# Summing the modulations' partial products on four column groups at once, with two accumulators

## The chip, the cores and the metric

The kernel runs on one core of a Trainium2 chip. The metric is the time on the device of one execution, in microseconds (us). TensorE multiplies matrices, VectorE and ScalarE work element by element, GpSimd does a few small things, and SyncE issues most of the DMAs. In the profile they are PE (PEld is its loading of weights), DVE, ACT, POOL and SP. Each engine takes its instructions strictly in the order in which the program lists them for it. An instruction waits for a semaphore where it needs another engine's result or a buffer that another engine still uses.

## The reference

The model is a hybrid of two layers over 512 tokens (256 of context, 256 latent) of 1024 channels. Every layer has nine modulation vectors for each of the two streams; the latent tokens are modulated by `c`, the context tokens by `c_ctx`:

```python
for l in range(DEPTH):                                  # DEPTH = 2
    ml = jnp.split((jax.nn.silu(c) @ ada_w[l] + ada_b[l])[:, None, :], N_MOD, axis=-1)
    mc = jnp.split(jax.nn.silu(c_ctx) @ ada_w[l] + ada_b[l], N_MOD, axis=-1)
    h = h + 0.5 * ml[2] * _swiglu(_modulate(_rms(h, ffn1_norm[l]), ml[0], ml[1]), ffn1_w13[l], ffn1_w2[l])
    ...                                                 # the context stream hc alike, with mc
    y_lat, y_ctx = _mixer(_modulate(_rms(h, mix_norm[l]), ml[3], ml[4]), ...)
    h = h + ml[5] * y_lat
    h = h + 0.5 * ml[8] * _swiglu(_modulate(_rms(h, ffn2_norm[l]), ml[6], ml[7]), ffn2_w13[l], ffn2_w2[l])
return _rms(h, final_norm)                              # of the latent stream
```

The change touches only how `silu(c) @ ada_w[l]` and `silu(c_ctx) @ ada_w[l]` are computed. One modulation is 1024 channels of two streams: for each stream a vector of 1024 numbers times a matrix of 1024 x 1024.

## The kernel before

**Stages.** The program runs through the two layers in order: first FFN of layer 0 (in the profiled execution until about 425 us), mixer of layer 0 (to about 1080), second FFN of layer 0 (to about 1455), first FFN of layer 1 (to about 1850), mixer of layer 1 (to about 2320), second FFN of layer 1. Activations lie with the channels on the partitions. Every large product (`mm3`, line 142) is made of three float32r products for each k tile of 128 channels: high part by high part, low by high, high by low. A weight tile of 1024 x 128 comes by one DMA of SyncE's queue (`raw`), ScalarE rounds it to its high part (`whi`, line 112), VectorE subtracts that from the raw tile for the low part (`wlo`, line 113), and TensorE then uses it for 24 products (8 k tiles by 3) of 512 columns. `whi` and `wlo` have three buffers each, so ScalarE can start on a tile when TensorE has left the tile three places earlier.

**Modulations.** Modulations 0 and 1 of layer 0 are made at the very start by TensorE (`ada_now`). The other sixteen (2 to 8 of layer 0, 0 to 8 of layer 1) are made beside the products of the FFNs by `ada`: seven in the first FFN of layer 0, six in its second, three in the first FFN of layer 1. A modulation is eight jobs. `beside` hands the jobs out evenly over 64 calls of `weights()`, so about one job follows each weight tile. A job loads 256 rows by 512 columns of `ada_w` (`adaw`, line 286, from the same pool of three buffers and the same SyncE queue as `raw`), and VectorE multiplies each row of it by the number of `silu(c)` for its partition and adds it up: `aacc` [128 partitions, 2 streams, 512 columns], two operations of line 293 for the first k tile and fourteen of line 295 for the other seven. Four jobs make one half (`r` = 0 or 1) of a modulation's 1024 columns.

What is then left is the sum over the 128 partitions. TensorE does it: a product with a 128 x 32 block of ones (line 301) puts the sum of every column on 32 rows of PSUM. A half has two such products, one for each stream, on the column groups `g = 2 * s + r` of the array (four groups of 32 columns); half 0 uses groups 0 and 2, and half 1 groups 1 and 3 of the same PSUM tile. The operands are plain float32, and each such product shows as two MATMUL records of 32 columns by 512 in the trace. After half 1 `modulation` copies the PSUM tile (ScalarE, line 239), transposes it in four pieces (TensorE, line 242), and VectorE adds the bias (line 249) and prepares the scales.

`aacc` has a single buffer (`bgp` is a pool of one). So the first operation of a half on VectorE cannot start before TensorE has done the previous half's two products:

```python
if k == 0:
    st.acc = self.bgp.tile([128, 2, 512], F32, tag="aacc", name="aacc")
...
if k == 6:
    if r == 0:
        st.ps = self.psx()
    for s in range(2):
        g = 2 * s + r
        nc.tensor.matmul(st.ps[32 * g:32 * g + 32, :], lhsT=self.ones[:, :32], rhs=st.acc[:, s],
                         start=True, stop=True, tile_position=(0, 32 * g))
```

**Order.** The order on each engine is settled when the program is built, by a scheduler of the framework that goes by the order of emission and by priorities; the two parts of a weight tile have a higher priority than the jobs. The order on SyncE's queue decides when weights and `ada_w` blocks are loaded.

**A relative.** `sums` in the mixer (line 931) does a sum over the partitions too, with the same shape of product (`sel`, 128 x 32, by 512 columns in plain float32), and issues four of them one behind the other on the four column groups. It is not changed, and its rows stand below as line 931.

## Time and profile before

| | |
|---|---|
| three runs | 2528.02, 2529.99, 2535.90 us |
| median of the runs | 2529.99 us |
| profiled execution: span from its first to its last instruction | 2526.3 us |
| profiled execution: what lies around the span | not recorded; the lowest run is 1.7 us above the span, the median 3.7 us |
| PE busy | 2427.5 us (96%) |
| DVE busy | 1776.3 us (70%) |
| ACT busy | 956.2 us (38%) |
| PE records of line 301 | 128, 37.1 us busy |
| DVE on the accumulations, lines 293 and 295 | 64 and 448 operations |

Busy time is the union of an engine's instructions. Matmuls overlap one another in the records (a product of 512 columns shows as some 0.39 us, and the next one starts 0.23 us later), so the time that TensorE spends on something is read from starts, not from the durations. In the rows below a timeline line gives the start in us from the start of the span, the length, the engine, the line of the program, the operation, what it writes and reads, the count of merged records, and in brackets how long the engine was idle before and what ended that.

### The profile page before, as it was taken

Reading aid. Unit: us, or ns where it says so; the run is one execution under the profiler, and the core shown is the slowest. Engines: PE = TensorE matmul, PEld = TensorE weight load, DVE = VectorE, ACT = ScalarE, POOL = GpSimd, SP = SyncE. Lnnn points to the kernel's source line nnn. Section 1 sums busy time; section 2 is a strip of 40 time slices with the busy share of each in tenths; the row PEclk is TensorE's granted clock in tenths of the full one; section 3 lists DMA queues with packets and bytes.
Section 4 is the critical chain, followed back from the end, with each engine's and each line's share of the span. In section 5 each row is a group of like instructions: output and inputs, shape, how many; then the busy total and the mean of one; then the engine's idle time right before and its main releaser. Section 6 shows DMA issues by size and latency. Waiting matters only on the chain. (4 is left out here: it accounts for less than half of the span.)

```text
span 2526.3 us, 38353 instructions
## 1 busy us (share of the span) xinstructions
PE 2427.5 (96%) x15099; PEld 2044.0 (81%) x15099; DVE 1776.3 (70%) x3023; ACT 956.2 (38%) x1578; POOL 51.5 (2%) x111
## 2 busy tenths in 40 slices
PE   7999999999999999999999999999988998978998
PEld 5777778787887887887777887777887897978998
DVE  4766767699999676576666564445468998966554
ACT  3222222435443643332222232222244556544443
POOL 0000000100000000000000000000010000000000
PEclk9999999999999999999999999999998998999999
DMA  8555555743653465355555544444466572356664
GB/s 252 167 162 166 172 174 175 167 134 109 209 142 115 144 217 161 119 151 161 158 153 163 152 118 126 125 125 127 127 163 180 168 212 82 94 186 174 196 185 137
DMA packets 566773, 394.61 MB, mean 156 GB/s; under 512 B 27704, under 2 KB 513218, under 8 KB 564930
## 3 DMA queue, kind: packets, MB, share of 16 engines
q1 hardware_dynamic: 555606, 371.33, 50.0%
q0 software_dynamic: 2304, 8.39, 1.7%
q10 hardware_dynamic: 8684, 12.45, 1.4%
q8 instruction: 118, 1.93, 0.3%
q14 instruction: 61, 0.50, 0.1%
HBM read 358.43 MB, written 33.69 MB: 155 GB/s over the span
## 5 line engine op out<-in xcount | busy, mean ns | idle before, releaser
L142 PE MATMUL pm<-nh,whi 128*128 128x512 f32 (+1 forms) x2544 | 910.6, 360 | 21.2 <-ACT whi L112 14.5
L142 PE MATMUL pm<-nh,wlo 128*128 128x512 f32 (+1 forms) x2544 | 905.4, 357 | 2.8 <-DVE wlo L113 2.2
L142 PE MATMUL pm<-nl,whi 128*128 128x512 f32 (+1 forms) x2544 | 905.9, 357 | 0.0
L112 ACT ACTIVATE whi<-raw 128x1024 fp32r<-128x1024 f32 (+1 forms) x450 | 469.0, 1044 | 1150.5 <-PE pm L142 892.4
L113 DVE TENSOR_TENSOR wlo<-raw,whi 128x1024 fp32r<-128x1024 f32 (+1 forms) x450 | 540.9, 1203 | 273.7 <-ACT whi L112 270.1
L142 PEld LDWEIGHTS pm<-nh,whi 128*128 128x128 f32 x2544 | 482.2, 190 | 121.7 <-ACT whi L112 32.5
L142 PEld LDWEIGHTS pm<-nh,wlo 128*128 128x128 f32 x2544 | 482.4, 190 | 79.8 <-DVE wlo L113 4.5
L142 PEld LDWEIGHTS pm<-nl,whi 128*128 128x128 f32 x2544 | 482.7, 190 | 73.1 <-DVE nl L376 1.0
L295 DVE SCALAR_TENSOR_TENSOR aacc<-adaw,sc,aacc 128x512 f32<-128x512 f32 x448 | 311.7, 746 | 111.7 <-DMA adaw<-ada_w_in 111.6
L825 DVE SCALAR_TENSOR_TENSOR cy<-cx,cdw,cy 128x512 f32<-128x512 f32 (+1 forms) x480 | 272.0, 612 | 1.3
L142 PE MATMUL pm<-gh,whi 128*128 128x512 f32 (+1 forms) x770 | 269.6, 350 | 1.7 <-DVE h L381 1.7
L142 PE MATMUL pm<-gl,whi 128*128 128x512 f32 (+1 forms) x770 | 267.6, 348 | 0.0
L142 PE MATMUL pm<-gh,wlo 128*128 128x512 f32 (+1 forms) x770 | 267.1, 347 | 0.0
L142 PEld LDWEIGHTS pm<-gh,whi 128*128 128x128 f32 x770 | 145.7, 189 | 30.5 <-ACT whi L112 6.7
L142 PEld LDWEIGHTS pm<-gl,whi 128*128 128x128 f32 x770 | 145.7, 189 | 18.4 <-issue 0.8
L142 PEld LDWEIGHTS pm<-gh,wlo 128*128 128x128 f32 x770 | 145.7, 189 | 18.1
L429 DVE TENSOR_TENSOR silu<-silu,pm 128x512 f32<-128x512 f32 (+1 forms) x88 | 54.5, 620 | 109.3 <-PE pm L142 100.9
L381 DVE SCALAR_TENSOR_TENSOR h<-pm,gate,h 128x256 f32<-128x256 f32 x80 | 36.5, 480 | 63.9 <-PE pm L142 63.6
L375 ACT ACTIVATE nh<-t,mods 128x256 fp32r<-128x256 f32 x88 | 39.9, 502 | 60.5 <-DVE t L372 60.4
L112 ACT ACTIVATE gh<-silu 128x512 fp32r<-128x512 f32 (+1 forms) x88 | 50.4, 573 | 12.1 <-DVE silu L429 12.1
L113 DVE TENSOR_TENSOR gl<-silu,gh 128x512 fp32r<-128x512 f32 (+1 forms) x88 | 54.4, 618 | 0.0
L142 PE MATMUL pm<-mh,whi 128*128 128x256 f32 (+1 forms) x152 | 47.9, 317 | 2.9 <-ACT mh L112 2.9
(248 smaller groups left out, 2382.6 us busy)
## 6 DMA issues: line engine op xcount, KB each, us to landing
raw<-ffn_w_in SPq DMA_DIRECT2D x208, 512.0 KB, 3.9
adaw<-ada_w_in SPq DMA_DIRECT2D x144, 512.0 KB, 4.4
raw<-w_in_in SPq DMA_DIRECT2D x130, 512.0 KB, 4.3
raw<-ffn_w_in SPq DMA_DIRECT2D x64, 448.0 KB, 4.2
R<-grow POOLq DMA_DIRECT2D x16, 512.0 KB, 13.6
raw<-conv_proj_in SPq DMA_DIRECT2D x16, 512.0 KB, 6.3
raw<-dn_proj_in SPq DMA_DIRECT2D x16, 512.0 KB
raw<-w_out_in SPq DMA_DIRECT2D x16, 512.0 KB, 4.0
```

Source lines behind the costliest of these rows:

```text
L112: nc.scalar.activation(out=hi, in_=x, func=AF.Copy)
L113: nc.vector.tensor_tensor(out=lo, in0=x, in1=hi.bitcast(F32), op=ALU.subtract)
L142: nc.tensor.matmul(ps, lhsT=u[:, j, :], rhs=v[:, k, tok], start=k == 0 and p == 0, stop=k == n - 1 and p == 2)
L295: nc.vector.scalar_tensor_tensor(out=st.acc[:, s], in0=wt[:, j], scalar=c, in1=st.acc[:, s], op0=ALU.mult, op1=ALU.add)
L375: nc.scalar.activation(out=nh[:, k, st], in_=t1, func=AF.Identity, bias=B)
L381: self.nc.vector.scalar_tensor_tensor(out=self.h[:, m, st], in0=ps[:, st], scalar=y.gate[:, q, m, s:s + 1], in1=self.h[:, m, st], op0=ALU. ...
L429: nc.vector.tensor_tensor(out=t, in0=t, in1=pb[:, tok], op=ALU.mult)
L825: nc.vector.scalar_tensor_tensor(out=dst, in0=src, scalar=w, in1=dst, op0=ALU.mult, op1=ALU.add)
```

## The change

Half 0 no longer issues its two products. Both halves keep their accumulator (`st.accs`), for which the tag `aacc` gets two buffers, and after half 1 all four products are issued in a row, on groups 0 to 3: half 0 and half 1 of stream 0, then half 0 and half 1 of stream 1. The PSUM tile is taken only there. (The file of the changed kernel also lost its comments; that moves the line numbers by one and changes nothing else.)

```diff
             if k == 0:
-                st.acc = self.bgp.tile([128, 2, 512], F32, tag="aacc", name="aacc")
+                st.acc = self.bgp.tile([128, 2, 512], F32, tag="aacc", name="aacc", bufs=2)
+                st.accs.append(st.acc)
...
-            if k == 6:
-                if r == 0:
-                    st.ps = self.psx()
-                for s in range(2):
-                    g = 2 * s + r
-                    nc.tensor.matmul(st.ps[32 * g:32 * g + 32, :], lhsT=self.ones[:, :32], rhs=st.acc[:, s],
+            if k == 6 and r == 1:
+                ps = self.psx()
+                for g in range(4):
+                    nc.tensor.matmul(ps[32 * g:32 * g + 32, :], lhsT=self.ones[:, :32], rhs=st.accs[g % 2][:, g // 2],
                                      start=True, stop=True, tile_position=(0, 32 * g))
-                if r == 1:
-                    self.modulation(y, (m,), st.ps, 0, 512, lambda pt: ...)
+                self.modulation(y, (m,), ps, 0, 512, lambda pt: ...)
...
-            st = SimpleNamespace()
+            st = SimpleNamespace(accs=[])
```

The change moves instructions on PE and DVE. On SP and POOL the order is the same as before, row for row, and on ACT six operations change places with a neighbour. On every engine the number of instructions is the same.

On PE, at the end of the first modulation that is made this way (modulation 2 of layer 0), this stands before; `aacc_825` is the accumulator of half 1, and half 0 has its own pair 97 rows earlier:

```order
L142 MATMUL pm_896<-nl_222,whi_899 128x512
L142 MATMUL pm_896<-nh_221,wlo_900 128x512
L301 MATMUL px_789<-aacc_825,ones_89 32x512 x2
L142 MATMUL pm_938<-nh_221,whi_941 128x512
L142 MATMUL pm_938<-nl_222,whi_941 128x512
```

And this stands there now:

```order
L142 MATMUL pm_893<-nl_222,whi_896 128x512
L142 MATMUL pm_893<-nh_221,wlo_897 128x512
L301 MATMUL px_948<-aacc_663,ones_89 32x512
L301 MATMUL px_948<-aacc_822,ones_89 32x512
L301 MATMUL px_948<-aacc_663,ones_89 32x512
L301 MATMUL px_948<-aacc_822,ones_89 32x512
L142 MATMUL pm_935<-nh_221,whi_938 128x512
L142 MATMUL pm_935<-nl_222,whi_938 128x512
```

The four stand at the same place among the products of line 142 as the pair of half 1 did (the numbers of the buffers differ by three), and where the pair of half 0 stood products of line 142 now follow one another. In fifteen of the sixteen modulations the four stand together so.

The sixteenth is modulation 8 of layer 0, at the end of the first FFN, where products of 256 columns run. Before, half 0 has a pair as elsewhere, and the two products of half 1 stand apart, on PE:

```order
L142 MATMUL pm_3061<-gh_611,whi_3076 128x256
L301 MATMUL px_2966<-aacc_2977,ones_89 32x512
L142 MATMUL pm_3061<-gl_612,whi_3076 128x256
L142 MATMUL pm_3061<-gh_611,wlo_3077 128x256
L142 MATMUL pm_3061<-gh_611,whi_3076 128x256
L142 MATMUL pm_3061<-gl_612,whi_3076 128x256
L142 MATMUL pm_3061<-gh_611,wlo_3077 128x256
L301 MATMUL px_2966<-aacc_2977,ones_89 32x512
L142 MATMUL pm_3061<-gh_611,whi_3088 128x256
```

Now the second and third of the four stand together and the fourth a little later, with the first (not in these rows) 34 rows ahead of the second:

```order
L142 MATMUL pm_3058<-gh_611,wlo_3074 128x256
L301 MATMUL px_3095<-aacc_2974,ones_89 32x512
L301 MATMUL px_3095<-aacc_2850,ones_89 32x512
L142 MATMUL pm_3058<-gh_611,whi_3073 128x256
L142 MATMUL pm_3058<-gl_612,whi_3073 128x256
L142 MATMUL pm_3058<-gh_611,wlo_3074 128x256
L142 MATMUL pm_3058<-gh_611,whi_3073 128x256
L142 MATMUL pm_3058<-gl_612,whi_3073 128x256
L301 MATMUL px_3095<-aacc_2974,ones_89 32x512
```

So in this modulation the products of line 301 interrupt the others three times now, and three times before (a pair and two single ones).

On DVE, between the halves of the first modulation, this stands before (`aacc_663` is half 0, `aacc_825` half 1):

```order
L295 SCALAR_TENSOR_TENSOR aacc_663<-adaw_783,sc_135,aacc_663 128x512 x3
L113 TENSOR_TENSOR wlo_820<-raw_817,whi_819 128x1024
L429 TENSOR_TENSOR silu_771<-silu_771,pm_734 128x512
L113 TENSOR_TENSOR wlo_863<-raw_860,whi_862 128x1024
L113 TENSOR_TENSOR gl_612<-silu_771,gh_611 128x512
L293 TENSOR_SCALAR aacc_825<-adaw_823,sc_135 128x512 x2
L295 SCALAR_TENSOR_TENSOR aacc_825<-adaw_823,sc_135,aacc_825 128x512 x2
L295 SCALAR_TENSOR_TENSOR aacc_825<-adaw_866,sc_135,aacc_825 128x512 x4
```

And this stands there now (`aacc_822` is half 1):

```order
L296 SCALAR_TENSOR_TENSOR aacc_663<-adaw_783,sc_135,aacc_663 128x512 x3
L294 TENSOR_SCALAR aacc_822<-adaw_820,sc_135 128x512
L113 TENSOR_TENSOR wlo_817<-raw_814,whi_816 128x1024
L294 TENSOR_SCALAR aacc_822<-adaw_820,sc_135 128x512
L296 SCALAR_TENSOR_TENSOR aacc_822<-adaw_820,sc_135,aacc_822 128x512 x2
L428 TENSOR_TENSOR silu_771<-silu_771,pm_734 128x512
L296 SCALAR_TENSOR_TENSOR aacc_822<-adaw_863,sc_135,aacc_822 128x512
L113 TENSOR_TENSOR wlo_860<-raw_857,whi_859 128x1024
```

Half 1's operations move up to stand directly behind half 0's, ahead of a product with `silu` and of one or two splits of weight tiles.

## Rows read from the trace of the kernel before

**Rows 1.** The page: busy time, share and instructions of each engine.

```profile
PE 2427.5 (96%) x15099; PEld 2044.0 (81%) x15099; DVE 1776.3 (70%) x3023; ACT 956.2 (38%) x1578; POOL 51.5 (2%) x111
```

**Rows 2.** Windows in three FFNs: stretch, length, each engine's busy time, clock, DMA.

```profile
60.00:296.00 236.00, 236.00 (x1015) 182.69 (x1014) 166.06 (x240) 66.13 (x86) 0.00 (x0) 1.00 0.55 164
1080.00:1350.00 270.00, 269.37 (x1207) 211.25 (x1207) 180.74 (x264) 78.00 (x103) 1.07 (x1) 1.00 0.52 154
1440.00:1710.00 270.00, 268.07 (x1291) 218.28 (x1290) 141.15 (x201) 81.25 (x111) 1.83 (x2) 1.00 0.42 123
```

**Rows 3.** Waits of PE from 60 to 425 us: us, times, longest.

```profile
PE px L301 <- DVE aacc L295: 1.4, 2, 0.8
```

**Rows 4.** Waits of all engines over the span.

```profile
ACT whi L112 <- PE pm L142: 892.4, 281, 8.9
DVE aacc L295 <- DMA adaw<-ada_w_in: 111.6, 55, 4.5
DVE aacc L293 <- PE px L301: 18.2, 11, 3.9
```

**Rows 5.** The tile aacc: records of line 301 and line 295, min/median/max in ns.

```profile
L295 DVE SCALAR_TENSOR_TENSOR aacc<-adaw,sc,aacc x448: 737/745/754, 64.4 to 1805.9; 128x512 f32<-128x512 f32 x150
L301 PE MATMUL px<-aacc,ones x128: 589/593/617, 84.0 to 1810.6; 128*32 128x512 f32 x128
```

**Rows 6.** Timeline of PE around the first pair.

```profile
83.48 0.39 PE L142 MATMUL pm<-nl,whi 128*128 128x512 f32 x1
83.71 0.39 PE L142 MATMUL pm<-nh,wlo 128*128 128x512 f32 x1
84.03 1.05 PE L301 MATMUL px<-aacc,ones 128*32 128x512 f32 x4
...
85.35 0.39 PE L142 MATMUL pm<-nl,whi 128*128 128x512 f32 x1
```

**Rows 7.** Timeline of PE around a single product, the first of modulation 8's half 1.

```profile
416.14 0.28 PE L142 MATMUL pm<-gh,whi 128*128 128x256 f32 x1
416.35 1.04 PE L301 MATMUL px<-aacc,ones 128*32 128x512 f32 x2
...
417.55 0.28 PE L142 MATMUL pm<-gh,wlo 128*128 128x256 f32 x1
417.67 0.28 PE L142 MATMUL pm<-gh,whi 128*128 128x256 f32 x1
```

**Rows 8.** Timeline of PE around four products together, line 931, twice.

```profile
571.67 0.39 PE L142 MATMUL pm<-nh,wlo 128*128 128x512 f32 x1
571.99 2.16 PE L931 MATMUL px<-sq,sel 128*32 128x512 f32 x8
...
574.42 0.39 PE L142 MATMUL pm<-nl,whi 128*128 128x512 f32 x1
...
596.35 0.39 PE L142 MATMUL pm<-nh,wlo 128*128 128x512 f32 x1
596.67 1.07 PE L931 MATMUL px<-sq,sel 128*32 128x512 f32 x8
...
598.01 0.40 PE L142 MATMUL pm<-nl,whi 128*128 128x512 f32 x1
```

**Rows 9.** Timeline of PE: the four pairs of a half 0 that took longer.

```profile
345.62 1.62 PE L301 MATMUL px<-aacc,ones 128*32 128x512 f32 x4 [0.67 <-DVE aacc L295]
...
394.83 1.62 PE L301 MATMUL px<-aacc,ones 128*32 128x512 f32 x4 [0.76 <-DVE aacc L295]
...
1104.63 1.49 PE L301 MATMUL px<-aacc,ones 128*32 128x512 f32 x4
...
1402.49 1.64 PE L301 MATMUL px<-aacc,ones 128*32 128x512 f32 x4
```

**Rows 10.** Timeline of ACT and DVE: the two parts of one weight tile.

```profile
78.36 1.06 ACT L112 ACTIVATE whi<-raw 128x1024 fp32r<-128x1024 f32 x1 [3.99 <-PE pm L142]
79.46 1.23 DVE L113 TENSOR_TENSOR wlo<-raw,whi 128x1024 fp32r<-128x1024 f32 x1 [0.45 <-ACT whi L112]
```

More of the change, by code (lines that the diff above doesn't have):

```diff
@@ L295, in job @@
                         nc.vector.scalar_tensor_tensor(out=st.acc[:, s], in0=wt[:, j], scalar=c, in1=st.acc[:, s], op0=ALU.mult, op1=ALU.add)
-            if k == 6:
-                if r == 0:
-                    st.ps = self.psx()
-                for s in range(2):
-                    g = 2 * s + r
-                    nc.tensor.matmul(st.ps[32 * g:32 * g + 32, :], lhsT=self.ones[:, :32], rhs=st.acc[:, s],
+            if k == 6 and r == 1:
+                ps = self.psx()
+                for g in range(4):
+                    nc.tensor.matmul(ps[32 * g:32 * g + 32, :], lhsT=self.ones[:, :32], rhs=st.accs[g % 2][:, g // 2],
                                      start=True, stop=True, tile_position=(0, 32 * g))
-                if r == 1:
-                    self.modulation(y, (m,), st.ps, 0, 512, lambda pt: pt.rearrange("p (j s g r) -> p g j s r", j=4, s=2, g=2)[:, :, :, :, 0])
+                self.modulation(y, (m,), ps, 0, 512, lambda pt: pt.rearrange("p (j s g r) -> p g j s r", j=4, s=2, g=2)[:, :, :, :, 0])
         jobs = []
         for m in mods:
-            st = SimpleNamespace()
+            st = SimpleNamespace(accs=[])
             jobs += [lambda m=m, r=r, k=k, st=st: job(m, r, k, st) for r in range(2) for k in (0, 2, 4, 6)]
```

## The prediction, made before the changed kernel ran

> **What bounds the kernel now.** I read the page's busy times first: TensorE is busy in 96% of the span, VectorE in 70% [rows 1]. A share over the whole span mixes FFNs with mixers, so next I took windows inside the three FFNs in which the sixteen modulations are made: TensorE is busy for 236.0 of 236 us, 269.4 of 270 and 268.1 of 270, at a granted clock of 1.00 throughout (its full 2.4 GHz), with VectorE at 166, 181 and 141 us and the DMA engines at 0.42 to 0.55 [rows 2]. The reader is to see that TensorE is the bound of these stretches and that nothing else is near it. The waits say the same from the other side: in the first FFN TensorE waited 1.4 us for an accumulator, and the answer has only one other row, of 0.6 us [rows 3]; ScalarE stood 892 us, in 281 pieces, waiting for TensorE to leave a weight buffer [rows 4]. Weights are ready ahead of TensorE, not behind it. So an instruction taken off TensorE there moves the end of the kernel by its whole cost, and the work of the accumulation on VectorE lies beside.
>
> Since matmul records overlap, a cost on TensorE is read from starts. I call one interruption of the products of line 142 by products of another shape a **break**, and measure it from the start of the last product ahead of it to the start of the second product behind it, less two ordinary steps. (The second one, because the step after the first product behind is still longer than usual.)
>
> **What one break costs.** Ordinary steps: 83.48 to 83.71, so 0.23 us for 512 columns [rows 6]; 417.55 to 417.67, 0.12 us for 256 columns [rows 7].
> - A pair of line 301: 83.71 to 85.35 is 1.64, less 0.46, is 1.18 us [rows 6].
> - A single product of line 301: 416.14 to 417.55 is 1.41, less 0.24, is 1.17 us [rows 7].
> - Four products of the same shape on four column groups, line 931: 596.35 to 598.01 is 1.66, less 0.46, is 1.20 us [rows 8].
>
> These are the rows on which the forecast rests: one, two or four products cost the same. A break costs 1.2 us, whatever it holds, as long as all operands are there when it begins. Where they are not, it costs more: the other four of line 931 stretched over 2.16 us because two of them came late, 571.67 to 574.42 is 2.75, less 0.46, is 2.29 us, that is 1.09 us more [rows 8].
>
> One rule of the Trainium skill weighs against issuing four: in "TensorE: Matmul & The Clock Gate", section "The cost: per-tile semaphore tail", the tail of a packed group grows by about 4.7 ns for a tile and 26.3 ns for each increment. Two more products with an increment each would by that page make a four dearer than a pair by an estimated 62 ns, 1.0 us for all sixteen, where the rows show 0.02 us; the sum would be 20.3 us instead of 21.0. The rows are of the same shape on the same engine, and I go by them.
>
> **The change part by part.**
> 1. *Breaks on TensorE.* Line 301 has 128 records [rows 5], two for a product, so 64 products. By the order on PE they make 33 breaks before: 31 pairs and two single ones (both of modulation 8 of layer 0). After, they make 18: fifteen fours, and modulation 8's four in three pieces. 15 breaks fewer, at 1.18 us, are 17.7 us. All lie in the FFNs, where TensorE is the bound, so they lie on the path.
> 2. *Fours for pairs.* A four is 0.02 us dearer than a pair; fifteen of them add 0.3 us.
> 3. *Stalls at half 0.* Four pairs of a half 0 took longer than the usual 1.05 us, because the last accumulations came only as TensorE arrived: 1.62 after 0.67 idle, 1.62 after 0.76 idle, 1.49 and 1.64 [rows 9]. The excess is 0.57 + 0.67, 0.57 + 0.76, 0.44 and 0.59, in sum 3.6 us. After the change TensorE doesn't come to half 0 at all at these points, so this goes too, unless the lateness is carried on to the four at the end of half 1. It should not be: TensorE now comes to line 301 only at half 1's place, about four weight tiles later, and half 1 need not wait for half 0's products any more. Before, every half had to wait for those of the half ahead, and VectorE stood 18.2 us in 11 places because of that [rows 4]. Now only the first half of a modulation has to, and on VectorE half 1 stands directly behind half 0.
> 4. *The second accumulator.* It takes 4 KB more of each partition and no instruction. No engine's instruction count changes.
> 5. *What is moved on VectorE.* Accumulations of half 1 now stand ahead of one or two splits (`wlo`), of products with `silu` and of the low parts of the FFN's inner activations. I cost this at nothing. What hides it is the lead of the weights: ScalarE starts on a tile at 78.36, the moment a buffer comes free, and VectorE is done with the low part at 80.69 [rows 10]. TensorE has two tiles of 24 products to do before it comes to that one, 48 steps of 0.23 us or 11.0 us from 78.36, so it is ready some 8.7 us early. Four accumulations of 0.745 us [rows 5] are 3.0 us; the cover is three times that. If it were gone, each such place would hold TensorE up by what is missing.
> 6. *What is moved on the queues.* SyncE's order is the same. Since half 1's blocks are used up somewhat earlier, its buffers come free earlier, and later loads can start earlier; with the DMA engines at about half [rows 2] I count this at nothing.
> 7. *Behind the four.* The copy, the transposes, and the vector operations of `modulation` stand where they stood, behind half 1's sums.
>
> The sum: 17.7 - 0.3 + 3.6 = 21.0 us off. The span was 2526.3 us, so 2505.3; the median of the runs lies 3.7 us above that span, so the median should come to 2529.99 - 21.0 = 2509.0 us, 0.83% less. What comes after each FFN is a chain of dependences that simply starts earlier, and I expect nothing to be given back there. A measurement of this kernel can tell a difference of about 0.3% (7.6 us) from none.
>
> **Rivals.**
> - *Lateness comes back in the fours.* TensorE reaches a four before half 1 is done, waits, and the four falls apart, since its second and fourth product need half 1. Price: up to 0.76 us of idle time [rows 9] and 1.09 us for a broken four [rows 8], 1.85 us each. If that happens in four modulations, as it did with four half 0s, 7.4 us of the gain go: 13.6 us off, 2516.4 us. For it: the residual parts of the FFNs, where the late pairs stand. Against it: point 3. Chance 0.10.
> - *The four don't run side by side.* The second two products would start when the first two are through. Price: up to the 1.05 us that the four records of a pair take [rows 6], so a four would save only 1.18 - 1.05 = 0.13 us against two pairs: 15 x 0.13 + 3.6 = 5.6 us off, 2524.4 us. Against it stand the eight records of line 931 in 1.07 us, hardly longer than a pair's four [rows 6, 8]. The Trainium skill has a rule from which this rival would follow: by "TensorE: Matmul & The Clock Gate", section "The mechanism" of its part on packing, the loading of weights overlaps running matmuls only where the row groups differ, and here all four products use all rows. By that rule, line 931 would not look as it does; the trace doesn't agree. Chance 0.02.
> - *VectorE becomes the bound of the FFNs.* Its 166 us of work in 236 would have to fit in some 231 [rows 2], which leaves 28% free. If it did bind, the breaks saved would be waited for elsewhere, and a gain of less than 7.6 us would remain, about 2526. Chance 0.04.
> - *Slower: accumulations that wait for their block hold up the weights.* VectorE takes its queue in order, and half 1's accumulations, now ahead of the splits, wait for blocks of `ada_w`: 111.6 us in 55 places before, the longest 4.5 us [rows 4]. If two such longest waits and four accumulations come ahead of a split, that is 12 us against a lead of 8.7, so TensorE loses 3.3 us in each of sixteen modulations, 53 us, which makes 32 us more than before: 2562 us. The point from which this decides is 10 us of delay ahead of a split (8.7 of lead and the 1.3 us that a modulation gains). Against it: SyncE loads in the same order, and the mean of those waits is 2.0 us. Chance 0.02.
>
> **How the numbers follow.** The forecast of 2509.0 us has 0.82. The range reaches up to the first rival, 2516.4, and 3 us further, since single runs lie from 2 us below to 6 us above the median; down it takes in the whole of what the runs scatter below the median (2 us) and 3 us for delays of the accumulations that would go unseen in point 3: 2504 to 2519 us. Faster by over 0.3% holds the forecast and the first rival, 0.92; within 0.3% the second and third, 0.06; slower 0.02.
>
> **What would show it.** In the profile of the changed kernel, line 301 should have its 128 records in 18 places on TensorE, each of fifteen fours about 1.07 us long, with 1.2 us between the steps around it; the excess of point 3 should be gone, and TensorE should not wait for an accumulator by more than about 1 us in all. TensorE's busy time should fall by some 20 us with the span. VectorE's wait of its first accumulation for line 301 should stay only at the first halves. The prediction is wrong if a four takes 2 us (second rival, or late operands, which the waits of TensorE for `aacc` would name), if the low parts of weights appear among TensorE's waits in the FFNs (the slower rival), or if the FFNs get shorter and a mixer longer by as much.

## The result, and the profile after

The changed kernel took 2514.92 us (median of four runs, 2511.57 to 2517.16), the kernel before beside it 2529.40 us (four runs). The ratio is 0.9937 with a 95% interval of 0.9925 to 0.9949. So 14.5 us were gained where 21.0 were forecast: the sign was right, the time lies inside the range of 2504 to 2519 us, and about a third of the forecast gain is missing. The profiled execution is the slowest of the four: 2517.16 us, with a span of 2515.4 us against 2526.3 before. That of the kernel before is, by its span, the fastest of its four (2528.02 us; the execution just named is 1.8 us longer than its span too). So the two profiles lie only 10.9 us apart, and what is missing in them is 3.6 us more than by the medians.

The page's busy line, then the three windows of [rows 2] (stretch, length, busy time of PE, PEld, DVE, ACT and POOL, clock, DMA share, GB/s), then the waits of ScalarE and VectorE that answer to [rows 4], all of the kernel after:

```profile
PE 2410.1 (96%) x15099; PEld 2043.3 (81%) x15099; DVE 1774.5 (71%) x3023; ACT 956.0 (38%) x1578; POOL 51.7 (2%) x111
```

```profile
60.00:296.00 236.00, 234.38 (x1028) 184.66 (x1027) 167.12 (x242) 67.95 (x88) 0.00 (x0) 1.00 0.59 168
1080.00:1350.00 270.00, 268.75 (x1211) 213.73 (x1211) 182.29 (x267) 80.35 (x106) 0.00 (x0) 1.00 0.56 161
1440.00:1710.00 270.00, 268.07 (x1294) 219.60 (x1293) 142.28 (x204) 81.09 (x110) 1.83 (x2) 1.00 0.43 125
```

```profile
ACT whi L112 <- PE pm L142: 857.7, 287, 8.9
DVE aacc L296 <- DMA adaw<-ada_w_in: 164.7, 74, 4.7
DVE aacc L294 <- DMA adaw<-ada_w_in: 28.6, 14, 4.0
```

TensorE has the same 15099 instructions and is busy for 17.4 us less than in [rows 1]; its span shrank by only 10.9 us, so 6.5 us of what it saved became idle time. In the first window there is 1.6 us of idle time that was not there in [rows 2]. TensorE is still the bound (ScalarE waits 857.7 us for it), and VectorE still has 69 us to spare in 236. VectorE's wait for TensorE of 18.2 us in [rows 4] is gone, since VectorE never has to wait for an accumulator to come free; in its place it waits longer for blocks of `ada_w`, 193 us against 115 (111.6 at line 295 [rows 4] and 3.3 at line 293; lines 294 and 296 are lines 293 and 295 of before).

Line 301 in the tile view (records, then min/median/max in ns), and one of the fours in TensorE's timeline:

```profile
L301 PE MATMUL px<-aacc,ones x128: 592/605/617, 106.9 to 1799.1; 128*32 128x512 f32 x128
```

```profile
106.30 0.40 PE L142 MATMUL pm<-nl,whi 128*128 128x512 f32 x1
106.53 0.40 PE L142 MATMUL pm<-nh,wlo 128*128 128x512 f32 x1
106.86 1.06 PE L301 MATMUL px<-aacc,ones 128*32 128x512 f32 x8
107.86 0.50 PE L142 MATMUL pm<-nh,whi 128*128 128x512 f32 x1
108.20 0.40 PE L142 MATMUL pm<-nl,whi 128*128 128x512 f32 x1
```

The eight records of a four take 1.06 us together, and the break is 106.53 to 108.20, 1.67, less 0.46, so 1.21 us: the forecast's 1.20.

**Where the gain went.** The products of line 142 are the same 11166 in the same order in both kernels, so the start of each can be set against its start before; where the difference jumps, time was gained or lost at that place. In the profiled execution of after:

| place | us |
|---|---|
| sixteen pairs of a half 0 gone: twelve at 1.17 to 1.21, the four late ones [rows 9] at 2.55, 2.59, 1.62 and 1.84 | -22.83 |
| modulation 8 of layer 0 in three breaks, without its pair of half 0 (sixteen pairs gone, fifteen breaks fewer) | +1.17 |
| its middle pair late | +0.71 |
| transposes of line 172 waiting for a load of vectors | +1.82 |
| transposes of line 242 waiting for ScalarE's copy, four places | +2.93 |
| one four broken by its late half 1 | +1.62 |
| mixer of layer 0 | +2.16 |
| before the first product, and all the rest | +1.59 |
| in all, at the last product | -10.83 |

The first two rows are the forecast's points 1 to 3, and they came out as -21.7 us against -21.0. What is missing was given back in other places. Three of them show in TensorE's waits (us in all, times, longest us), here first from 60 to 425 us, then from 1080 to 1800 us:

```profile
PE px L172 <- DMA rows<-conv_dw_in: 1.6, 1, 1.6
PE px L301 <- DVE aacc L296: 0.6, 1, 0.6
...
PE px L242 <- ACT adas L239: 0.4, 1, 0.4
```

```profile
PE px L242 <- ACT adas L239: 1.7, 3, 0.6
...
PE px L301 <- DVE aacc L296: 0.2, 1, 0.2
```

*The copy.* ScalarE's timeline, and TensorE's, behind the first four of the second FFN:

```profile
1129.36 1.06 ACT L112 ACTIVATE whi<-raw 128x1024 fp32r<-128x1024 f32 x1 [3.91 <-DMA raw<-ffn_w_in]
1130.32 0.62 ACT L112 ACTIVATE gh<-silu 128x512 fp32r<-128x512 f32 x1
1130.84 0.58 ACT L239 ACTIVATE adas<-px 128x512 f32<-128x512 f32 x1
```

```profile
1128.60 1.06 PE L301 MATMUL px<-aacc,ones 128*32 128x512 f32 x8
...
1130.64 0.40 PE L142 MATMUL pm<-nl,whi 128*128 128x512 f32 x1
1131.47 0.66 PE L242 MATMUL px<-ident,adas 128*128 128x128 f32 x4 [0.44 <-ACT adas L239]
1131.88 0.48 PE L142 MATMUL pm<-nh,wlo 128*128 128x512 f32 x1
```

The copy stands behind `whi` and `gh` on ScalarE, and `whi` came late, since its weights did. By the order on PE the transposes stood seven products behind the last pair in fourteen of the sixteen modulations before; now they stand four or five behind the four in fifteen. That is 0.5 to 0.7 us less for the copy. The copy itself is later too: before, it ended 0.64 to 0.68 us behind the last product of line 301 in all sixteen modulations; in the four places that cost time here it ended 1.44 to 1.94 us behind the four. TensorE stood idle for 0.37 to 0.62 us at them; with the two or three more products of before in between, at most 0.2 us would be left by these rows (an estimate).

*The load.* ScalarE's own queue issues the small loads of a layer's vectors (ACTq), in order with its other instructions:

```profile
142.01 1.06 ACT L112 ACTIVATE whi<-raw 128x1024 fp32r<-128x1024 f32 x1 [4.05 <-PE pm L142]
145.06 0.63 ACT L112 ACTIVATE gh<-silu 128x512 fp32r<-128x512 f32 x1 [1.99 <-DVE silu L428]
145.15 0.35 ACTq L169 DMA_DIRECT2D rows<-conv_dw_in  x1
```

```profile
141.69 2.74 DVE L296 SCALAR_TENSOR_TENSOR aacc<-adaw,sc,aacc 128x512 f32<-128x512 f32 x4 [2.90 <-DMA adaw<-ada_w_in]
144.35 0.68 DVE L428 TENSOR_TENSOR silu<-silu,pm 128x512 f32<-128x512 f32 x1
```

```profile
146.83 0.39 PE L142 MATMUL pm<-nh,wlo 128*128 128x512 f32 x1
148.84 0.29 PE L172 MATMUL px<-ident,rows 120*128 120x120 f32 x1 [1.62 <-DMA rows<-conv_dw_in]
```

VectorE waited 2.90 us for a block, its four accumulations stood ahead of the `silu` product, `gh` waited for that, and the load stood behind `gh`. It was issued at 145.15, and at 145.27 in the kernel before: the same time. But TensorE, with two breaks less and these transposes two products earlier in its order, is there 2.4 us earlier than before (146.83 plus a step of 0.23, against 149.45). In the kernel before:

```profile
145.27 0.36 ACTq L169 DMA_DIRECT2D rows<-conv_dw_in  x1
149.45 0.27 PE L172 MATMUL px<-ident,rows 120*128 120x120 f32 x1
```

*The late four.* TensorE's timeline at the place where the first rival came true:

```profile
1419.55 0.39 PE L142 MATMUL pm<-gh,wlo 128*128 128x512 f32 x1
1419.87 1.04 PE L301 MATMUL px<-aacc,ones 128*32 128x512 f32 x2
1421.10 1.71 PE L301 MATMUL px<-aacc,ones 128*32 128x512 f32 x6 [0.19 <-DVE aacc L296]
1422.74 0.50 PE L142 MATMUL pm<-gh,whi 128*128 128x512 f32 x1
```

The first product, of half 0, could go; the other three waited for half 1. It cost 1.62 us, where the rival had 1.85.

### The profile page after: what moved, and what is told of

It reads as the page before. It is cut to its first block, busy times and chain, and to the rows that moved or that the text cites. A ratio compares the mean times of both kernels' runs of the same rounds, so it can differ in the third digit from the quotient of the medians.

```text
span 2515.4 us, 38318 instructions
## 1 busy us (share of the span) xinstructions
PE 2410.1 (96%) x15099; PEld 2043.3 (81%) x15099; DVE 1774.5 (71%) x3023; ACT 956.0 (38%) x1578; POOL 51.7 (2%) x111
## 5 line engine op out<-in xcount | busy, mean ns | idle before, releaser
L142 PE MATMUL pm<-nh,whi 128*128 128x512 f32 (+1 forms) x2544 | 907.8, 359 | 23.2 <-ACT whi L112 16.3
L112 ACT ACTIVATE whi<-raw 128x1024 fp32r<-128x1024 f32 (+1 forms) x450 | 469.1, 1044 | 1109.3 <-PE pm L142 857.7
L142 PEld LDWEIGHTS pm<-gl,whi 128*128 128x128 f32 x770 | 145.7, 189 | 17.6
```

The lines of the kernel that those rows point to most:

```text
L112: nc.scalar.activation(out=hi, in_=x, func=AF.Copy)
L142: nc.tensor.matmul(ps, lhsT=u[:, j, :], rhs=v[:, k, tok], start=k == 0 and p == 0, stop=k == n - 1 and p == 2)
```

## Experiments

The theory after the result: the change takes some 22 us off TensorE as forecast, and then TensorE arrives earlier than work that hangs on `ada_w` blocks and on loads (copy, load, late half 1). The rivals: the breaks saved are worth less than they seem, or the second accumulator, not the breaks, makes the difference. Each run stands against its own runs of the kernel before on the same chip. e0, e1, e2 and e5 shared a chip, so did e6 to e9, and so did e10 to e13; "beside it" means the changed kernel of the same group.

### The changed kernel again, three times

No edit.

> The changed kernel once more, in five rounds, to fix the size of the gain: its first four runs lie between 2511.6 and 2517.2 us. By my account of the first trace the forecast 21.0 us shrank to 10.9 us in the profiled execution, of which some 2 us fell into the first mixer, which the change does not touch. If that part is scatter, the median should come to 2511 to 2515 us, 15 to 18 us under the kernel before; if the mixers really became slower, it stays at 2515 to 2518.

> The changed kernel itself, beside the next three on one chip. If the 7.7 us between its two measurements so far (2514.9 and 2507.2) is the scatter of single executions and chips, it comes out anywhere from 2507 to 2515. If the gain of 21 us is there in the breaks and only now and then given back by waits, the products of line 142 that were next to a removed pair start 1.07 us earlier at each of them in this trace too, and what the total lacks to 21 us is found in waits with a name. The rival, that the breaks saved were worth less than forecast, would show as steps of less than 1 us.

> The changed kernel once more, as the measure for the runs beside it: between 2507 and 2515, with its single runs spread over some 10 us, if late blocks and late weights meet TensorE in some executions and not in others.

| | after | before | ratio, 95% |
|---|---|---|---|
| first | 2514.92 | 2529.40 | 0.9937 [0.9925, 0.9949] |
| e0_after_again | 2507.18 | 2526.83 | 0.9923 [0.9911, 0.9935] |
| e6_after_third | 2512.35 | 2529.18 | 0.9931 [0.9913, 0.9949] |
| e13_after_fourth | 2510.27 | 2530.02 | 0.9926 [0.9913, 0.9938] |

The gains are 14.5, 19.7, 16.8 and 19.8 us. The second measurement came out below both times that were expected of it, the third and the fourth inside theirs. All twenty runs of after have a median of 2510.0 us (2504.6 to 2517.5), all fifty-nine of before beside them 2528.8 (2523.0 to 2535.9): 18.8 us. The four profiled executions place by place, against the one of before, in us:

| | first | again | third | fourth |
|---|---|---|---|---|
| sixteen pairs gone, and the third break | -21.7 | -21.7 | -21.7 | -21.7 |
| modulation 8's middle pair late | +0.7 | +0.2 | +0.8 | +0.5 |
| the load of line 172 | +1.8 | +0.1 | +1.4 | +1.5 |
| the copy, four places | +2.9 | +0.3 | +2.9 | +1.3 |
| the late four | +1.6 | +0.1 | +1.1 | +1.2 |
| mixer of layer 0 | +2.2 | +0.3 | +1.5 | +1.2 |
| all else | +1.6 | -0.6 | +1.0 | -0.3 |
| in all | -10.8 | -21.2 | -13.0 | -16.3 |

The gain in the breaks is the same each time, to a few hundredths. What differs is what is given back, always at the same places, and in one execution almost nothing was. The mixer of layer 0 is no place of the change: against the same execution of before it is 0.7 us longer in e1 and 3.4 us in e10, which are kernels with pairs.

### e1_pairs_two_acc: the second accumulator alone

```diff
-                st.acc = self.bgp.tile([128, 2, 512], F32, tag="aacc", name="aacc")
+                st.acc = self.bgp.tile([128, 2, 512], F32, tag="aacc", name="aacc", bufs=2)
```

This is an edit of the kernel before; pairs stay where they were.

> The kernel before with two buffers for aacc and nothing else: 33 breaks on TensorE as before, each half with its pair. Theory (the gain is the breaks that are saved): only the late half 0s of rows 9 can get better, so 0 to 4 us under the kernel before, 2526 to 2530 us. Rival (the gain comes from the second accumulator, which frees VectorE from waiting for TensorE): 10 us or more under the kernel before, as the changed kernel.

2531.68 us, ratio 1.0019 [1.0008, 1.0030]: 4.9 us slower. The theory's time was missed by 2 us on the slow side; the rival, that the accumulator is the gain, fell. In the profiled execution, 4.8 us longer than that of before, the loss is mostly one place, TensorE's timeline (and below it windows on the same stretch, in the columns above):

```profile
1403.18 0.39 PE L142 MATMUL pm<-gh,whi 128*128 128x512 f32 x1
1406.59 2.12 PE L301 MATMUL px<-aacc,ones 128*32 128x512 f32 x4 [3.02 <-DVE aacc L295]
1408.63 0.79 PE L142 MATMUL pm<-gl,whi 128*128 128x512 f32 x1
1409.22 0.63 PE L142 MATMUL pm<-gh,wlo 128*128 128x512 f32 x1
1409.65 0.63 PE L142 MATMUL pm<-gh,whi 128*128 128x512 f32 x1
```

```profile
1402.00:1406.00 4.00, 1.57 (x7) 0.95 (x6) 4.00 (x8) 0.81 (x2) 0.00 (x0) 1.00 0.29 83
1408.00:1410.00 2.00, 2.00 (x4) 1.16 (x4) 0.00 (x0) 0.00 (x0) 0.00 (x0) 0.50 0.78 219
```

A pair of a half 0 is late by 3.02 us here, and the place costs 4.7 us more than before, where its pair was late as well [rows 9]: after that idle time the granted clock is 0.50 (1.2 GHz of 2.4), and a step takes 0.43 us in place of 0.23 until about 1411. The pairs of half 0 meet late accumulations with two accumulators as with one. Why this one is later than before was not followed, nor whether it is so in the other nine executions.

### e5_extra_break: the price of one more break

```diff
+            if k == 2 and r == 1:
+                px = self.psx()
+                for g in range(4):
+                    nc.tensor.matmul(px[32 * g:32 * g + 32, :], lhsT=self.ones[:, :32], rhs=st.accs[0][:, g // 2],
+                                     start=True, stop=True, tile_position=(0, 32 * g))
```

An edit of the changed kernel: sixteen more fours, of half 0 alone, whose results nobody reads. Fifteen stand in breaks of their own; that of modulation 8 joins a break that is there already. So the kernel has 33 breaks, as many as the kernel before.

> The changed kernel with one more break in each modulation: four products of line 301 on the first half's accumulator, into a PSUM tile that nothing reads, in the second job of half 1, where their operands have long been there. Theory (a break of four costs 1.2 us): 16 x 1.2 = 19 us over the changed kernel, 2534 us, slower than the kernel before by 4. If a four cost as much as two pairs one behind the other (2.2 us), 35 us over, 2550 us. If TensorE had slack there, less than 10 us over.

2527.19 us, ratio to before 1.0001 [0.9992, 1.0009], so 20.0 us over the changed kernel on the same chip: 1.25 us for each of the sixteen. The first of them in TensorE's timeline:

```profile
94.42 0.39 PE L142 MATMUL pm<-nh,wlo 128*128 128x512 f32 x1
94.73 1.06 PE L300 MATMUL px<-aacc,ones 128*32 128x512 f32 x8
...
96.06 0.39 PE L142 MATMUL pm<-nl,whi 128*128 128x512 f32 x1
```

94.42 to 96.06 is 1.64, less 0.46, is 1.18 us. Against the products of line 142 each of the fifteen shows as one jump of 1.08 to 1.09 us and some 0.1 us at the next step. With as many breaks as the kernel before, the changed kernel takes as long. That is the direct measurement of the forecast's 1.2 us; the 1.25 us hold the scatter of two medians besides.

### e11_four_twice: what a break is made of

```diff
-                for g in range(4):
+                for g in (0, 1, 2, 3, 0, 1, 2, 3):
```

> The changed kernel with the four products of each modulation issued twice in the same break, so eight products in place of four, with the same result. If a break is mostly a fixed price of changing the shape, sixteen doubled fours cost little, under 5 us in all. If the first four take about 1.05 us to stream and the change of shape is the small rest, they cost 0.85 to 1.05 us each, 14 to 17 us over the changed kernel; the steps around each break show it as 0.85 to 1.05 us more. The forecast's sum holds either way, since it counts breaks of one, two or four products.

2530.68 us, ratio 1.0004 [0.9995, 1.0013], 20.4 us over the changed kernel on the same chip; 14 to 17 were expected. TensorE's timeline at the first of them:

```profile
105.76 0.39 PE L142 MATMUL pm<-nh,wlo 128*128 128x512 f32 x1
106.08 1.92 PE L301 MATMUL px<-aacc,ones 128*32 128x512 f32 x16
107.93 0.50 PE L142 MATMUL pm<-nh,whi 128*128 128x512 f32 x1
```

The second four adds 0.86 us (1.92 against 1.06), and 0.85 to 0.88 at each other place that stands whole; that is as expected, and sixteen of them are 13.8 us. The rest is not the price of a four: in the profiled execution the transposes of one place waited 3.79 us for the copy, which cost 5.4 us more there than in e13. Those two make 19.2 us, where the two profiled executions lie 17.6 us apart and the medians 20.4; whether that place is late in the other executions is not known. If the first four streams as long as the second, a break of 1.2 us is some 0.86 us in which one, two or four products stream side by side, and some 0.34 us for the change of shape (an estimate). The Trainium skill says in "TensorEngine Tiling (Array Packing)", section "Key Properties", that changing the tiling mode drains TensorE. The 0.34 us that are left over agree with it.

### e2_transposes_later: a test that moved more than it should

```diff
-                self.modulation(y, (m,), ps, 0, 512, ...)
+                later.append(self.modulation(y, (m,), ps, 0, 512, ...))
...
+        jobs.append(lambda: later.pop()())
```

Each modulation's transposes are issued at the start of the next job, and one job is added for the last.

> The changed kernel, with the four transposes of a modulation and what follows them emitted one job later (about a weight tile), ScalarE's copy where it was. Theory (the order on PE puts the transposes 4 or 5 products behind the four instead of 7, so that TensorE now waits for ScalarE's copy at four places, 0.4 to 0.6 us each, and pays 0.6 to 0.8 us with what follows): these waits go, 2 to 4 us under the changed kernel. Rival (what is missing from the forecast lies in the fours themselves or in the mixers): within 1 us of the changed kernel.

2518.16 us, ratio 0.9961 [0.9948, 0.9974]: 11.0 us over the changed kernel, where 2 to 4 under it were expected. The added job raised the rate at which jobs are handed out, and most of the fours moved 24 to 66 products ahead. There TensorE met accumulations that were not done: 5.6 us of idle time in three places where fours broke apart, which came out 3.8, 5.0 and 4.5 us longer than in e0 against the products of line 142. So the run says nothing on the copy, but it shows the first rival at work: how late a four stands decides whether it is whole, and the margin in the residual parts of the FFNs is small.

### e7_transposes_later_clean: the same without the added job

```diff
+                later.append(self.modulation(y, (m,), ps, 0, 512, ...))
+                if m == mods[-1]:
+                    later.pop()()
```

> The changed kernel, with the transposes of a modulation issued with the first accumulation of the next one (24 or 48 products behind the four in place of 4 or 5), the last modulation of each FFN as before, and no job added, so that all the fours stay in their places. If the transposes wait for the copy of the sums because the change put them nearer behind the four, the waits of TensorE at line 242 for line 239 go in all places but six, and the time is 0.5 to 3 us under the changed kernel on the same chip (four such waits cost 0.6 to 0.8 us each in its first profile, one in its second). The rival, that these waits stand for some other lateness that shows at the next place anyway, gives the same time.

2510.19 us against 2512.35 of the changed kernel on the same chip (ratios to before 0.9925 [0.9910, 0.9939] and 0.9931 [0.9913, 0.9949]): 2.2 us less, as expected in size, though the intervals overlap and the two are not told apart by it. TensorE's waits from 1075 to 1790 us, first of the changed kernel beside it (e6_after_third), then of this one (line 246 is line 242):

```profile
PE px L242 <- ACT adas L239: 2.3, 3, 1.0
```

```profile
PE px L246 <- ACT adas L239: 0.4, 1, 0.4
```

At the two copy places whose transposes moved 24 products on (about 1130 and 1260 us) the changed kernel beside it lost 0.56 and 1.16 us, this one 0.03 and 0.01. The one wait left is at a place whose transposes did not move (about 1370 us). That looks like the theory, but it does not show it: in this execution the copies at the two moved places were on time, ending 1.03 and 0.95 us behind their fours, where they ended 1.64 and 2.25 us behind them in e6. In e0 copies that ended 0.95 us behind the four cost nothing there, with the transposes where the change put them. So the move was not put to the test, and that the nearness of the transposes exposes a late copy is read from the order and the waits of the first execution (*The copy*, above).

### e8_no_blocks and e10_no_blocks_before: both kernels without the blocks

```diff
-            wt = self.rawp.tile([128, 2, 512], F32, tag="raw", name="adaw")
-            nc.sync.dma_start(out=wt, in_=w[k * 128:(k + 2) * 128, c0:c0 + 512]...)
+        block = self.ones.unsqueeze(1).to_broadcast([128, 4, 128])
```

The accumulations read a block of ones with factors of zero, so the loads and the products with the modulation's weights are left out; the same edit on the changed kernel (e8) and on the kernel before (e10).

> The changed kernel without the blocks of ada_w: the accumulations of the sixteen modulations read a constant in place of a loaded block and add it with a factor of zero, so the loads and the products with the modulation's weights are left out, and all instructions of VectorE and TensorE stay. VectorE then never waits for a block, and a weight tile never waits behind one. If late blocks and late weights are what is given back, no four is late, no accumulation waits, the mean lead of weights grows, and the time is 2 to 5 us under the changed kernel on the same chip. If the lateness costs nothing when it runs as in the second measurement, the two are the same within 1.5 us. A time of over 8 us less would say that the traffic of the blocks slows the FFNs in itself, in before and after alike.

> The kernel before without the blocks of ada_w, in the same way as the run without blocks of the changed kernel (the loads and the products with the modulation's weights are left out; all instructions of TensorE and VectorE stay). Its products of line 301 stand in 32 pairs, the changed kernel's without blocks in 16 fours. If the gain is in the number of breaks alone, 16 of them at 1.18 us less 16 x 0.02 us, it is 18.6 us above the changed kernel without blocks, which stood 25.2 us under its kernel before, so some 7 us under its kernel before; no pair of a half 0 is late. If it is the lateness of blocks that the four gets rid of, the distance is under 10 us. If blocks hurt the changed kernel alone, this one is as fast as the kernel before, within 2 us.

The changed kernel without blocks: 2503.94 us (2502.1 to 2507.4), ratio 0.9902 [0.9886, 0.9918], 8.4 us under the changed kernel on the same chip, more than the 2 to 5 expected; the two intervals just touch. TensorE's whole list of waits from 60 to 425 us and from 1075 to 1790 us is

```profile
PE pm L142 <- DVE h L378: 0.6, 1, 0.6
PE px L347 <- POOL rs L340: 0.5, 1, 0.5
```

```profile
PE px L347 <- POOL rs L340: 1.1, 2, 0.6
PE pm L142 <- DVE h L378: 0.6, 1, 0.6
```

with no copy, no load, no accumulator among them: all the places at which time was given back in the FFNs are at zero (0.0, 0.0 and -0.3 us), and modulation 8's four holds together. That makes 16 breaks where the changed kernel has 18, so some 2.4 of the 8.4 us are breaks. The mixer of layer 0 has +2.35 us here too, so that one is not made by late blocks.

The kernel before without blocks: 2526.00 us, ratio 0.9979 [0.9970, 0.9988], so 4.0 us under its own before, where some 7 were expected; the late pairs of half 0 lost 3.8 us of their price, and modulation 8's half 1 is one pair (32 breaks in place of 33, some 1.2 us). The distance between the two kernels without blocks is 0.0077, 19.5 us, against the 18.6 that sixteen breaks at 1.18 us less 16 x 0.02 come to. With both intervals that is 19.5 us give or take some 5. So the gain of the breaks does not hang on the lateness of blocks. The loads of the blocks cost the changed kernel some 6 us beside the breaks that it saves without them, and the kernel before some 3. The 8.4 us of e8 alone would have spoken for a traffic that slows both kernels alike; the 4.0 us of e10 speak against it.

### e9_order_and_queue and e12_later_and_queue: edits on what is given back

```diff
-                for g in range(4):
+                for g in (0, 2, 1, 3):
...
-        net.small = net.nc.scalar
+        net.small = net.nc.gpsimd
```

The first edit is of e9 alone, the second of both. e12 also has the later transposes of e7.

> The changed kernel with two small edits: the four products issued in the order half 0, half 0, half 1, half 1, and the small loads of vectors of a layer on GpSimd's queue in place of ScalarE's. By the first the late half 1 leaves two products that can go at once, which takes nothing off a break whose operands are all there. By the second no load stands behind a split of gh that waits for VectorE, so the wait of 1.6 us at line 172 in the first profile of the changed kernel can't come back. Theory: 0 to 2 us under the changed kernel on the same chip. Rival: GpSimd starts a transfer later than ScalarE, and other vectors come late: up to 2 us over it.

> The changed kernel with the transposes issued with the next modulation's first accumulation and the small loads of vectors on GpSimd's queue in place of ScalarE's. If the waits for the copy (2.3 us idle in the last profile, up to 4 us between the products of line 142) and the wait at line 172 (1.2 and 1.6 us) are what it gives back most, it is 2 to 4 us under the changed kernel on the same chip, with the highest of its runs under 2512. Rival: the scatter comes from late blocks wherever they show, and the time is the changed kernel's within 1.5 us.

e9: 2508.93 us, ratio 0.9919 [0.9905, 0.9933], 3.4 us under the changed kernel beside it (0 to 2 were expected). e12: 2508.90 us, 0.9921 [0.9908, 0.9935], 1.4 us under it (2 to 4 were expected), its highest run 2511.98 as forecast. In both, the transposes of line 172 at 147 us wait for nothing, +0.0 us in place of +1.4 and +1.5 in the changed kernel beside them. In e9 that is a test of the load: `gh` waited 1.73 us for VectorE there, nearly as in the first execution, but the load was issued at 142.06, before `gh`, landed at 144.11, and TensorE came to it at 146.84. In e12 the two moved copy places are at zero again, with copies that are on time as in e7 (1.11 and 1.03 us behind the four), and its late four cost 2.8 us, which had been 0.1 to 1.6. Most of what the profiled executions of e9 and e12 lie under those of e6 and e13 (8.6 and 3.6 us) falls into the mixer of layer 1, 5.5 and 4.5 us shorter there than in before against 0.4 longer and 0.8 shorter in e6 and e13; that was not followed. All intervals overlap with the changed kernel's, so none of the three is shown to be faster than it. The order of the four in e9 left modulation 8 in three breaks and did nothing that could be seen.

## Why the prediction was right, and where it was short

**Points 1 and 2 (breaks, fours for pairs): right.** Twelve undisturbed pairs of half 0 brought 1.17 to 1.21 us each in four traces, e5 charged 1.25 us for putting a break back (1.18 in its trace), and a four takes 1.06 us as [rows 8] said.

**Point 3 (stalls at half 0): right.** The four late pairs brought 8.6 us where four plain ones bring 4.7: 3.9 us against the forecast's 3.6. What made them late were the blocks, and not the wait for the one accumulator that the point names: without blocks (e10) their price is gone, though VectorE still waits 16.7 us for TensorE to leave it. That the lateness would not come back in the fours was half right: of these four modulations two had fours that were whole and on time; the third is modulation 8, whose middle pair was late (0.2 to 0.8 us), and the fourth has the broken four (1.62, 0.14, 1.07 and 1.20 us in the four executions).

**Point 4 (accumulator): not quite nothing.** In the kernel before it cost 4.9 us by itself (e1), in the profiled execution mostly through one late pair; in the changed kernel no such pair exists.

**Point 5 (accumulations ahead of the splits): right.** TensorE never waited for a low part in these stretches, although VectorE's waits for blocks grew from 115 to 193 us. The slower rival fell with that. But the cover was named for the weights alone: two others also waited behind those accumulations, `gh` with the load behind it, and half 1 itself.

**Point 6 (queues): the step that failed first.** SyncE's order was the same, as it said; but ScalarE's queue carries the loads of vectors, and there the point looked at nothing. In the first execution one load is issued no earlier than before and TensorE comes 2.4 us earlier; it cost 0.1 to 1.8 us in four executions. The 0.1 us are of e0, where it was issued at 143.19; in the other three it was issued at 144.43 to 145.27. After, it landed 3.6 us after its issue; the same from 145.27 in the kernel before would be 148.9, an estimate, and TensorE used it there at 149.45. That is some 0.6 us of cover, against two breaks of 1.18 us saved ahead of it. That the queue is the cause is shown by e9.

**Point 7 ("stand where they stood"): wrong.** The transposes moved from seven to four or five products behind the sums, and in six places the copy stands behind one more instruction on ScalarE. The order on the engines showed it; the prediction looked at the vector operations alone. Price: 0.3 to 2.9 us in four executions, and only where the copy came late. The waits show that TensorE met the copy too early; that the old distance would have covered it is an estimate, since e7 did not test it.

**The first rival** (0.10, 2516.4 us) is nearest to the first measurement in time, but by its own mechanism only two of its four places came true, and cheaper than its 1.85 us each (0.71 and 1.62 us). Most of what is given back in the FFNs came by ways that no rival named: the copy and the load. **The second** fell: the eight records of a four take 1.06 us, and all sixteen pairs gone are gone for good. The Trainium skill's rule behind it ("TensorE: Matmul & The Clock Gate", section "The mechanism") would let the loading of weights overlap only where the row groups differ; the traces do not agree for these four: in the four at 106.86 us the second product's weights are loaded at 106.87 us, while the first runs until 107.48. The 62 ns that the prediction worked out from the Trainium skill's semaphore tail (same page, section "The cost: per-tile semaphore tail") rest on two increments more for a four. The trace has none more: in every four that stands whole two of the eight records update a semaphore, as two of the four do in a pair. With two more products and no more increments the Trainium skill's figures come to an estimated 9 ns, and the 0.01 to 0.02 us between a pair and a four agree with that. **The third** fell with VectorE's 167 us in 236. One reading of the prediction was wrong and changed nothing in its sum: in the broken four of [rows 8] one product came late and not two (three start together at 571.99 us, the fourth at 573.10).

Against the forecast of 2509.0 us the first median is 5.9 us too long, the median of all twenty runs 1.0 us. In gain the forecast was 21.0 and all runs give 18.8. That the first time lies inside the range is in part luck: the range was drawn up to the first rival, and it was mostly the copy, the load and a mixer that filled it. What stays open: the 0.3 to 2.4 us in the mixer of layer 0 and the differences in that of layer 1, which differ between executions of each kernel and were not followed further, and why blocks and weights come later in some executions than in others.

## What to carry to other kernels

A few small products between large ones cost their break, not their number: count interruptions of the engine that binds, price one from starts, and put together what can be put together. Then ask of each thing that the engine meets next how much earlier the engine will be there: a load, a copy or an accumulator that is not made earlier takes part of the gain back, here up to 1.8 us at one place. Look at the order on every queue, ScalarE's among them, before writing "stands where it stood".

## What the runs showed of the hardware

- A break of float32 products of 128 x 32 by 512 columns between products of 128 x 128 costs 1.2 us for one, two or four on different column groups; a second four in the same break costs 0.86 us more (e11).
- A late operand can cost more than its wait. After 3.02 us of idle time the granted clock was 0.50, a step took 0.43 us in place of 0.23, and the place cost 4.7 us more than before (e1). After 1.95 us of idle time that ended at 363 us in e2 it was 0.50 too, from 364 to 366 us; after 2.31 us that ended at 1367 us in the same execution, and after the 1.62 us at 147 us in the changed kernel, it stayed at 1.00. So the length of one idle stretch does not tell what it costs.
- Executions of one and the same kernel differ by 13 us (2504.6 to 2517.5 in twenty runs of after). At the places of the FFNs listed above the profiled executions of after differ by 6 us between them. That the blocks make the scatter is not shown: without them four runs lay within 5.3 us (e8) and ten within 8.9 us (e10), and five runs of e0 with them within 4.2 us.
